# Rotary embedding on one core: one pass per 4 MB slab for the first six slabs, halves for the last two, and the sin products kept as bf16 in the slab's own memory

## The chip, the cores and the metric

The kernel runs on one core of one Trainium2 chip. The metric is the device time of one execution in microseconds; the median of five runs stands for a kernel. Beside these runs there is one profiled execution, and all durations of single instructions come from it.

## The reference

The input is 16 batches of 512 positions of 1024 numbers in fp32, seen as 16 heads of 64. Each head's first and second halves are rotated against each other with tables of cos and sin that depend on the position and on the place in the half, and that all batches and heads share.

```python
x = x.reshape(batch, seq, num_heads, head_dim)
x1, x2 = x[..., :half_dim], x[..., half_dim:]
cos = cos[None, :, None, :]
sin = sin[None, :, None, :]
rotated = np.concatenate([
    x1 * cos - x2 * sin,
    x1 * sin + x2 * cos
], axis=-1)
```

The output has the input's size: 33.55 MB are read and 33.55 MB written, and the two tables have 64 KB each.

## The kernel before, in words

Two batches make a slab: 1024 positions, eight to a partition (`rpp` is 8), so a slab is a tile of 128 partitions by 8192 fp32 numbers, 4 MB, and each partition's 32 KB are contiguous in memory. There are eight slabs, and five slots (`slots`) for them in SBUF. Five loads are issued on SP's queue at the start. A slab's result is written back over its own input in the slot, and one DMA on ScalarE's queue (L139) stores the whole slab. Load s + 5 (L65) takes the slot of slab s, so SP waits for store s to land before it issues that load.

The tables come in through two DMAs from POOL (L75), are cast to bf16 (L92), and four small matmuls with a selection matrix (L96) give every partition the rows of its own eight positions; L102 to L106 lay them out as `tab`: 8 rows of cos, then 8 rows of [sin, -sin], each row 64 numbers wide. They are used for all heads by a step of zero.

The work goes over a list of passes, `passes`: a slab has two, of four positions (`rows`) or 4096 numbers a partition each. A pass has five steps:

- ScalarE casts the half slab to bf16 into a tile `xb` (L117, in `cast`).
- VectorE multiplies `xb` by the sin rows into a tile `t2` (L130; the profile calls it t), and then `xb` by the cos rows in place (L130 again).
- VectorE adds `t2` to `xb`, with the halves of each head exchanged by a negative step (L133).
- ScalarE casts `xb` back to fp32 into the slab (L137).
- After a slab's second pass ScalarE issues the store (L139).

ScalarE's order is set by the loop: the cast of pass i + 1 stands ahead of the cast back of pass i. All engines take their instructions in order. `xb` has three buffers of 8 KB a partition and `t2` two of 8 KB; with five slabs of 32 KB that makes 200 KB a partition.

Loads go through one DMA queue and stores through another, and both run on the same 16 DMA engines.

Of the kernel before, what the change touches and what calls it, by code (L numbers as in the profile page):

```python
# [2 lines left out]

# [4 lines left out]


@with_exitstack  # L10
def kernel(
    ctx: ExitStack,
    tc: tile.TileContext,
    x: bass.AP,
    cos: bass.AP,
    sin: bass.AP,
    num_heads: int,
    out: bass.AP,
):
    nc = tc.nc  # L20
    P = nc.NUM_PARTITIONS

    batch, seq, dim = x.shape
    nh = num_heads
    hd = dim // nh
    half = hd // 2
    bf16 = mybir.dt.bfloat16
    f32 = mybir.dt.float32

    nb = 2  # L30
    slots = 5
    nslabs = batch // nb
    rpp = nb * seq // P
    W = rpp * dim
    SP = seq // rpp
    rows = 4
    PW = rows * dim
    TW = rpp * half

    out_flat = out.rearrange("b s h d -> b s (h d)")  # L40

    singles = ctx.enter_context(tc.tile_pool(name="singles", bufs=1))
    slabs = ctx.enter_context(tc.tile_pool(name="slabs", bufs=slots))
    tpool = ctx.enter_context(tc.tile_pool(name="tpool", bufs=3))
    t2pool = ctx.enter_context(tc.tile_pool(name="t2pool", bufs=2))
    psum = ctx.enter_context(tc.tile_pool(
        name="psum", bufs=1, space=bass.MemoryType.PSUM))


    def dram(t, s, a=0, n=W):  # L50
        return bass.AP(tensor=t.tensor, offset=t.offset + s * nb * seq * dim + a,
                       ap=[[W, P], [1, n]])


    def view(t, offset, *dims):
        return dataclasses.replace(t, offset=t.offset + offset,
                                   ap=[t.ap[0], *[list(d) for d in dims]])


    slab = {}  # L60


    def load(s):
        slab[s] = slabs.tile([P, W], f32, tag="slab", name="slab")
        nc.sync.dma_start(out=slab[s], in_=dram(x, s))  # L65


    load(0)


    TR = seq // P
    G = rpp // TR
    raw = singles.tile([P, 2 * TR * half], f32, tag="raw")
    for i, src in enumerate((cos, sin)):
        nc.gpsimd.dma_start(out=view(raw, i * TR * half, (1, TR * half)), in_=bass.AP(  # L75
            tensor=src.tensor, offset=src.offset,
            ap=[[TR * half, P], [1, TR * half]]))

    for s in range(1, slots):
        load(s)  # L80


    pick = singles.tile([P, G * P], bf16, tag="pick")
    nc.gpsimd.memset(pick, 0.0)  # L84
    for g in range(G):
        part = view(pick, g * P, (SP, P // SP), (1, SP))
        nc.gpsimd.affine_select(  # L87
            out=part, in_=part, compare_op=mybir.AluOpType.not_equal, fill=1.0,
            base=-g, pattern=[[0, P // SP], [-G, SP]], channel_multiplier=1)

    tab1 = singles.tile([P, 2 * TR * half], bf16, tag="tab1")
    nc.vector.tensor_copy(out=tab1, in_=raw)  # L92
    acc = psum.tile([P, 2 * TW], f32, tag="acc")
    for i in range(2):
        for g in range(G):
            nc.tensor.matmul(view(acc, i * TW + g * TR * half, (1, TR * half)),  # L96
                             view(pick, g * P, (1, P)),
                             view(tab1, i * TR * half, (1, TR * half)),
                             start=True, stop=True)

    tab = singles.tile([P, 2 * rpp * hd], bf16, tag="tab")
    nc.vector.tensor_copy(out=view(tab, 0, (hd, 2 * rpp), (1, half)),  # L102
                          in_=view(acc, 0, (half, 2 * rpp), (1, half)))
    nc.vector.tensor_copy(out=view(tab, half, (hd, rpp), (1, half)),  # L104
                          in_=view(acc, 0, (half, rpp), (1, half)))
    nc.vector.tensor_scalar_mul(  # L106
        out=view(tab, rpp * hd + half, (hd, rpp), (1, half)),
        in0=view(acc, TW, (half, rpp), (1, half)), scalar1=-1.0)


    xb = {}


    def cast(u):
        s, k = u
        xb[u] = tpool.tile([P, PW], bf16, tag="xb", name="xb")
        nc.scalar.copy(out=xb[u], in_=view(slab[s], k * PW, (1, PW)))  # L117

    passes = [(s, k) for s in range(nslabs) for k in range(rpp // rows)]
    cast(passes[0])
    for i, u in enumerate(passes):
        if i + 1 < len(passes):
            cast(passes[i + 1])
        s, k = u
        xs, xu = slab[s], xb.pop(u)
        t2 = t2pool.tile([P, PW], bf16, tag="t2")
        for t, a in ((t2, rpp * hd), (xu, 0)):
            nc.vector.tensor_mul(  # L130
                out=t, in0=xu,
                in1=view(tab, a + k * rows * hd, (hd, rows), (0, nh), (1, hd)))
        nc.vector.tensor_add(  # L133
            out=xu, in0=xu,
            in1=view(t2, half, (hd, rows * nh), (-half, 2), (1, half)))

        nc.scalar.copy(out=view(xs, k * PW, (1, PW)), in_=xu)  # L137
        if k == rpp // rows - 1:
            nc.scalar.dma_start(out=dram(out_flat, s), in_=xs)  # L139
            if s + slots < nslabs:  # L140
                load(s + slots)


# [1 line left out]
_INS = ['x', 'cos', 'sin', 'num_heads']  # L145
_OUTS = [((16, 512, 16, 64), 'float32')]

_NUMBERS = {'num_heads': 16}


# [26 lines left out]
```

## Time and profile before

| What | Value |
|---|---|
| Median of 5 runs | 162.46 us (162.37 to 163.0) |
| Profiled execution | 162.55 us |
| Span of its instructions | 160.5 us |
| VectorE busy | 111.3 us, 69% of the span, 52 instructions |
| ScalarE busy | 114.8 us, 72% of the span, 33 instructions |
| Moved by DMA | 67.24 MB, mean 419 GB/s over the span |
| Load, issue to landing, median | 27.5 us |
| Store, issue to landing, median | 28.5 us |
| Issue of the stores 0 to 7 | 34.46, 48.64, 62.82, 77.00, 93.77, 113.13, 132.50, 146.68 us |
| Issue of the loads 5, 6, 7 | 59.03, 78.57, 97.86 us |

The span is the time from the program's first instruction to its last event; the profiled execution's own time is about 2 us longer, and that difference lies around the span. A share of the span is a mean over stages, so an engine at 70% may be the limit in one stage and idle in another. The time from issue to landing of a load or a store contains the time in which it lies in its queue behind others: a slab's packets themselves take about 10 us when its queue has the DMA engines alone, and about 19 us when loads and stores share them.

### The profile page before, as it was taken

The page shows a single profiled execution, that of the slowest core. Times are in us where ns is not written, and L with a number is a line of the kernel's source. Part 1 is how long each engine was busy: PE and PEld are TensorE (multiplying, and loading weights), DVE is VectorE, ACT ScalarE, POOL GpSimd, SP SyncE. Part 2 cuts the span into 40 slices and gives each one's busy share as a digit, 9 for nine tenths or more (in the row PEclk, how much of TensorE's full clock was granted, in tenths as well). Part 3 has the DMA queues.
Part 4 walks back from the last instruction along what each step waited for, and adds up shares of the span by engine and source line. Part 5 has one row for each costly group of instructions (what it writes and reads, how often), then busy time and mean ns, then how long its engine had stood idle before and what let it go on. Part 6 is the DMA issues. An engine that isn't in the chain of part 4 may idle for free.

```text
span 160.5 us, 182 instructions
## 1 busy us (share of the span) xinstructions
PE 0.6 (0%) x4; PEld 0.4 (0%) x4; DVE 111.3 (69%) x52; ACT 114.8 (72%) x33; POOL 2.3 (1%) x9
## 2 busy tenths in 40 slices
PE   0010000000000000000000000000000000000000
PEld 0000000000000000000000000000000000000000
DVE  0003799999999999999997499906998089960000
ACT  3006939899999999999994999159990799735000
POOL 5000000000000000000000000000000000000000
DMA  7999999999999999999999999999999999999994
GB/s 237 425 417 392 482 433 392 433 474 351 441 392 441 474 392 392 474 441 392 466 449 392 441 457 408 441 457 408 400 482 425 392 474 441 392 474 441 392 457 196
DMA packets 2368, 67.24 MB, mean 419 GB/s; under 512 B 288, under 2 KB 288, under 8 KB 320
## 3 DMA queue, kind: packets, MB, share of 16 engines
q1 hardware_dynamic: 1152, 33.55, 49.4%
q10 hardware_dynamic: 1152, 33.55, 48.4%
q0 software_dynamic: 64, 0.13, 0.2%
HBM read 33.69 MB, written 33.55 MB: 419 GB/s over the span
## 4 chain that ended last, share of the span: by engine, by line
DMA 47%; ACT 25%; DVE 13%; issue 6%; ACTq 0%; SPq 0%
DMA slab<-in_x_dram 25%; DMA out_dram<-slab 22%; ACT slab L137 16%; ACT xb L117 9%; DVE xb L130 4%; DVE t L130 4%; DVE xb L133 4%; ACTq L137 0%; SPq L65 0%
## 5 line engine op out<-in xcount | busy, mean ns | idle before, releaser
L117 ACT CAST xb<-slab 128x4096 bf16<-128x4096 f32 x16 | 57.6, 3604 | 27.1 <-DMA slab<-in_x_dram 27.1
L137 ACT CAST slab<-xb 128x4096 f32<-128x4096 bf16 x16 | 57.7, 3605 | 4.1 <-DVE xb L133 3.9
L130 DVE TENSOR_TENSOR t<-xb,tab 128x4096 bf16<-128x4096 bf16 x16 | 36.7, 2291 | 18.7 <-ACT xb L117 18.3
L133 DVE TENSOR_TENSOR xb<-xb,t 128x4096 bf16<-128x4096 bf16 x16 | 36.7, 2292 | 0.5
L130 DVE TENSOR_TENSOR xb<-xb,tab 128x4096 bf16<-128x4096 bf16 x16 | 36.7, 2291 | 0.5
L92 DVE CAST tab<-raw 128x256 bf16<-128x256 f32 x1 | 0.3, 294 | 11.2 <-DMA raw<-in_sin_dram 11.2
L117 ACT ACT_TABLE_LOAD x1 | 1.3, 1283 | 0.7 <-PEq L158 0.7
L102 DVE CAST tab<-acc 128x512 bf16<-128x512 f32 x1 | 0.7, 691 | 0.7 <-PE acc L96 0.7
L75 POOL DMA_DIRECT2D raw<-in_cos_dram x1 | 0.7, 677 | 0.8 <-POOLq L158 0.8
L96 PE MATMUL acc<-tab,pick 128*128 128x128 bf16 x4 | 0.6, 300 | 11.5 <-DVE tab L92 11.5
L87 POOL TENSOR_SCALAR_AFFINE_SELECT pick<-pick 128x128 bf16<-128x128 bf16 x2 | 0.5, 289 | 0.1
L75 POOL DMA_DIRECT2D raw<-in_sin_dram x1 | 0.5, 537 | 0.0
L96 PEld LDWEIGHTS <-pick 128*128 128x128 bf16 x4 | 0.4, 124 | 11.4 <-issue 8.3
L106 DVE TENSOR_SCALAR tab<-acc 128x256 bf16<-128x256 f32 x1 | 0.4, 415 | 0.0
L104 DVE CAST tab<-acc 128x256 bf16<-128x256 f32 x1 | 0.4, 414 | 0.0
L84 POOL MEMSET pick<- 128x256 bf16 x1 | 0.3, 331 | 0.0
L158 POOL MEMSET const-float32-0.0<- 128x1 f32 x1 | 0.1, 99 | 0.2 <-issue 0.2
L158 POOL MEMSET const-bfloat16-1.0<- 128x1 bf16 x1 | 0.1, 102 | 0.0
L158 POOL MEMSET const-uint8-127<- 128x1 uint8 x1 | 0.1, 102 | 0.0
L158 POOL MEMSET const-float32-1.0<- 128x1 f32 x1 | 0.1, 99 | 0.0
## 6 DMA issues: line engine op xcount, KB each, us to landing
slab<-in_x_dram SPq DMA_DIRECT2D x8, 4096.0 KB, 27.5
out_dram<-slab ACTq DMA_DIRECT2D x8, 4096.0 KB, 28.5
raw<-in_cos_dram POOLq DMA_DIRECT2D x1, 64.0 KB, 7.2
raw<-in_sin_dram POOLq DMA_DIRECT2D x1, 64.0 KB, 9.2
```

Source lines behind the costliest of these rows:

```text
L75: nc.gpsimd.dma_start(out=view(raw, i * TR * half, (1, TR * half)), in_=bass.AP(tensor=src.tensor, offset=src.offset, ap=[[TR * half, P], ...
L84: nc.gpsimd.memset(pick, 0.0)
L87: nc.gpsimd.affine_select(out=part, in_=part, compare_op=mybir.AluOpType.not_equal, fill=1.0, base=-g, pattern=[[0, P // SP], [-G, SP]], c ...
L96: nc.tensor.matmul(view(acc, i * TW + g * TR * half, (1, TR * half)), view(pick, g * P, (1, P)), view(tab1, i * TR * half, (1, TR * half)) ...
L102: nc.vector.tensor_copy(out=view(tab, 0, (hd, 2 * rpp), (1, half)), in_=view(acc, 0, (half, 2 * rpp), (1, half)))
L104: nc.vector.tensor_copy(out=view(tab, half, (hd, rpp), (1, half)), in_=view(acc, 0, (half, rpp), (1, half)))
L106: nc.vector.tensor_scalar_mul(out=view(tab, rpp * hd + half, (hd, rpp), (1, half)), in0=view(acc, TW, (half, rpp), (1, half)), scalar1=-1.0)
L117: nc.scalar.copy(out=xb[u], in_=view(slab[s], k * PW, (1, PW)))
L130: nc.vector.tensor_mul(out=t, in0=xu, in1=view(tab, a + k * rows * hd, (hd, rows), (0, nh), (1, hd)))
L133: nc.vector.tensor_add(out=xu, in0=xu, in1=view(t2, half, (hd, rows * nh), (-half, 2), (1, half)))
L137: nc.scalar.copy(out=view(xs, k * PW, (1, PW)), in_=xu)
L158: nc = _bacc.Bacc("TRN2", target_bir_lowering=False, num_devices=1)
```

## The change

The first six slabs are done in one pass of 8192 numbers a partition; the last two keep two passes of 4096 each. `xb` becomes a tile of a whole slab (16 KB a partition) with two buffers, allocated when a slab's first pass begins. The tile `t2` goes: the sin product is written as bf16 into the first half of the bytes of the very part of the slab that has just been cast, and the cast back overwrites it with the result. A slab is still loaded by one DMA and stored by one DMA, in five slots. The tables' loads, from POOL, are the same in both kernels.

```diff
-    rows = 4
-    PW = rows * dim
...
-    tpool = ctx.enter_context(tc.tile_pool(name="tpool", bufs=3))
-    t2pool = ctx.enter_context(tc.tile_pool(name="t2pool", bufs=2))
+    xpool = ctx.enter_context(tc.tile_pool(name="xpool", bufs=2))
...
     def cast(u):
-        s, k = u
-        xb[u] = tpool.tile([P, PW], bf16, tag="xb", name="xb")
-        nc.scalar.copy(out=xb[u], in_=view(slab[s], k * PW, (1, PW)))
+        s, r, n = u
+        if r == 0:
+            xb[s] = xpool.tile([P, W], bf16, tag="xb", name="xb")
+        nc.scalar.copy(out=view(xb[s], r * dim, (1, n * dim)),
+                       in_=view(slab[s], r * dim, (1, n * dim)))
...
-    passes = [(s, k) for s in range(nslabs) for k in range(rpp // rows)]
+    passes = []
+    for s in range(nslabs):
+        n = rpp if s < nslabs - 2 else rpp // 2
+        passes += [(s, r, n) for r in range(0, rpp, n)]
...
     cast(passes[0])
-    for i, u in enumerate(passes):
+    for i, (s, r, n) in enumerate(passes):
         if i + 1 < len(passes):
             cast(passes[i + 1])
-        s, k = u
-        xs, xu = slab[s], xb.pop(u)
-        t2 = t2pool.tile([P, PW], bf16, tag="t2")
+        xs = view(slab[s], r * dim, (1, n * dim))
+        xu = view(xb[s], r * dim, (1, n * dim))
+
+        t2 = view(slab[s].bitcast(bf16), 2 * r * dim, (1, n * dim))
         for t, a in ((t2, rpp * hd), (xu, 0)):
             nc.vector.tensor_mul(
                 out=t, in0=xu,
-                in1=view(tab, a + k * rows * hd, (hd, rows), (0, nh), (1, hd)))
+                in1=view(tab, a + r * hd, (hd, n), (0, nh), (1, hd)))
         nc.vector.tensor_add(
-            out=xu, in0=xu,
-            in1=view(t2, half, (hd, rows * nh), (-half, 2), (1, half)))
+            out=xu, in0=xu, in1=view(t2, half, (hd, n * nh), (-half, 2), (1, half)))
 
-        nc.scalar.copy(out=view(xs, k * PW, (1, PW)), in_=xu)
-        if k == rpp // rows - 1:
-            nc.scalar.dma_start(out=dram(out_flat, s), in_=xs)
+        nc.scalar.copy(out=xs, in_=xu)
+        if r + n == rpp:
+            nc.scalar.dma_start(out=dram(out_flat, s), in_=slab[s])
             if s + slots < nslabs:
                 load(s + slots)
```

## The prediction

> **What bounds the kernel now.** I read the forty slices first, because they say at once whether any engine or the transfers are busy throughout.
>
> ```profile
> DVE  0003799999999999999997499906998089960000
> ACT  3006939899999999999994999159990799735000
> DMA  7999999999999999999999999999999999999994
> GB/s 237 425 417 392 482 433 392 433 474 351 441 392 441 474 392 392 474 441 392 466 449 392 441 457 408 441 457 408 400 482 425 392 474 441 392 474 441 392 457 196
> ```
>
> VectorE and ScalarE have holes; the 16 DMA engines have none between the first and the last slice. The table of DMA queues puts a price on this.
>
> ```profile
> q1 hardware_dynamic: 1152, 33.55, 49.4%
> q10 hardware_dynamic: 1152, 33.55, 48.4%
> q0 software_dynamic: 64, 0.13, 0.2%
> ```
>
> Together 98.0% of 160.5 us. q1 holds the loads, q10 the stores, the same bytes each. The stores' share is 0.484 x 160.5 = 77.7 us, or 9.7 us for each of eight 4 MB slabs; if loads cost the same, 16 slabs need 155.4 us. So only 160.5 - 155.4 = 5.1 us of the span is not plain transfer. In the trace's packet records the first packet starts at 1.75 and the last ends at 159.2; that makes 1.75 + 1.25 us at the two ends and about 2.1 us inside. Next, stretches of the span side by side tell where those 2.1 us are (columns: stretch, length, busy time by engine, clock, DMA share, GB/s).
>
> ```profile
> 10.00:35.00 25.00, 0.59 (x4) 0.32 (x3) 19.36 (x12) 18.40 (x6) 0.00 (x0) 1.00 1.02 440
> 35.00:40.00 5.00, 0.00 (x0) 0.00 (x0) 4.59 (x3) 5.00 (x2) 0.00 (x0) 1.00 0.96 360
> 60.00:125.00 65.00, 0.00 (x0) 0.00 (x0) 54.18 (x24) 52.38 (x15) 0.00 (x0) 1.00 1.00 432
> 125.00:150.00 25.00, 0.00 (x0) 0.00 (x0) 13.75 (x6) 17.83 (x5) 0.00 (x0) 1.00 0.99 429
> ```
>
> Loads alone (10 to 35), both directions (60 to 125) and stores alone (125 to 150) run at one rate, within what cutting at a packet's start costs; it doesn't matter how the two are mixed. The only dip is at 35 to 40, where the first store, issued at 34.46, joins the loads. By packets: a 32 KB packet takes 1.213 us in the steady state, and what packets took beyond this, for each engine, was 0.71 us at 0 to 4, 0.64 us at 36 to 40, 0.18 us at 56 to 60, and about 0.1 us over 4 to 34; the tables' packets are another 0.3 us. That is the 2.1 us. After 60 it is nil.
>
> The chain of waits and the end of ScalarE's timeline say what the last store waited for.
>
> ```profile
> DMA 47%; ACT 25%; DVE 13%; issue 6%; ACTq 0%; SPq 0%
> ```
>
> ```profile
> 125.36 3.60 ACT L117 CAST xb<-slab 128x4096 bf16<-128x4096 f32 x1 [5.15 <-DMA slab<-in_x_dram]
> 143.04 3.60 ACT L137 CAST slab<-xb 128x4096 f32<-128x4096 bf16 x1 [3.46 <-DVE xb L133]
> 146.68 0.34 ACTq L139 DMA_DIRECT2D out_dram<-slab  x1
> ```
>
> The chain's 38% of ACT and DVE must not be taken for time to be had: it is a path through one slab's work, with the DMA engines full beside it. Slab 7 lands at 125.34, its store is issued at 146.68, and its packets start at 148.95, 9.68 us after those of slab 6, which is the plain pitch. The last store came just in time; an earlier issue ends nothing earlier.
>
> **What the Trainium skill says.** "DMA: Bandwidth & Descriptors", section Queues, rings and completion order: each DMA engine takes turns among the rows that have work, packet by packet. The trace agrees: with both queues active each moves about 216 GB/s, alone 433. The same page under Specifications gives 435 GB/s as the ceiling on the SBUF side; 432 here is that ceiling. "SBUF — State Buffer", section Who interferes with whom: DMAs have ports of their own and don't contend with compute engines; packets of 1.213 us with VectorE at 9 tenths agree. "VectorE: DVE Perf Modes", section on the perf-mode tier table: a bf16 tensor_tensor in SBUF runs at two elements a cycle; here 4096 elements took 2.291 us, which is that.
>
> **The change part by part.** The order of instructions of the changed program on each engine gives the counts; the durations come from the costliest groups of the kernel before (busy us, mean ns of one, idle time before them).
>
> ```profile
> L117 ACT CAST xb<-slab 128x4096 bf16<-128x4096 f32 x16 | 57.6, 3604 | 27.1 <-DMA slab<-in_x_dram 27.1
> L137 ACT CAST slab<-xb 128x4096 f32<-128x4096 bf16 x16 | 57.7, 3605 | 4.1 <-DVE xb L133 3.9
> L130 DVE TENSOR_TENSOR t<-xb,tab 128x4096 bf16<-128x4096 bf16 x16 | 36.7, 2291 | 18.7 <-ACT xb L117 18.3
> ```
>
> 1. Fewer, longer instructions. 32 casts of 4096 become 12 of 8192 and 8 of 4096; 48 vector operations become 18 of 8192 and 12 of 4096. No cast of 8192 is in the trace: at most 2 x 3.605 = 7.21 us, at least the 186 ns + 0.833 ns an element of "ScalarE: Activation LUTs" (What ACT_TABLE_LOAD costs), 7.01 us; its 3.60 at 4096 is the trace's. A vector operation of 8192: at most 4.58, and by (cycles + 151)/0.96 GHz of the vector page's TRN2 errata section, which gives 2.291 at 4096, 4.42 us. I take 7.01 and 4.42. VectorE's slab goes from 13.7 to 13.3 us, ScalarE's from 14.4 to 14.0. Busy time falls by 2 to 3 us on each, and none of it is on the path that sets the end: the DMA engines need 2 x 9.7 = 19.4 us a slab.
>
> 2. The first store goes out later. Slab 0 lands at 13.53 as before. Cast 13.55 to 20.6, three operations to 34.0, cast back to 41.0, store at about 41.1 instead of 34.46. These 6.6 us are covered by loads: five are queued from the start, and at 9.7 us each and a first end at 13 they last to 51.8 alone. SP's queue holds nothing but loads, so nothing else is passed.
>
> 3. What follows in the load queue. Load 5 waits for store 0's landing. First store packet 4.0 us after its issue (34.46 to 38.49), so 45.1. Load 4, begun at 42.2, has by then moved 2.9 us at the full rate, the rest goes at half: done at 58.7. Store 0 does its last 2.9 us at the full rate: data out at 61.6, landed near 62; before, 58.94. Load 5 is issued then, with first packets 1.0 us later (as load 0) to 4 us later (as store 0). So from 58.7 to 63 or 66 the load queue is empty, which before it never was (load 5 issued at 59.03, load 4's packets end at 65.7). Store 1, issued at 55.2, fills the engines: 6.4 us of cover. Without it the gap would cost up to its 4 to 7 us.
>
> 4. The rest. Sharing from 64: load 5 ends at 83.4, load 6 at 102.8, load 7 at 122.2, landed 123.8 (before 125.34): what loads gained early, stores give up. ScalarE keeps its order: the next pass's cast stands ahead of this pass's cast back, so it can block on a load while a finished slab waits. Stores 2 to 4 are issued near 69, 84 and 99, each before the one ahead has ended.
>
> 5. The end. Slabs 6 and 7 go in halves, as all did before. Cast of 7's first half at 123.8; behind it on ScalarE stand the cast back of 6's second half, the second cast, and two casts back; the last of these waits for VectorE till 141.5. Store 7 is issued at about 145.2, 1.5 us ahead of before, with store 6's packets lasting to about 149. No gain: the queue is full.
>
> 6. Sin products in the slab's memory. The write must follow the cast that reads that memory, but the product waits for that very cast's output anyway; the cast back already waits for the addition. The halves touch disjoint bytes, and each half's first product has its own wait on ScalarE, so none waits for the other half's cast. Slots stay five, so no load may start earlier. Cost: nothing, hidden by DMA; point C tells when not.
>
> 7. Tables: POOL's list is the same in both programs, line numbers apart. Nothing.
>
> Sum against the profiled execution: span 160.5; ends unchanged; 155.4 of transfer unchanged; the start's 0.71, the tables' 0.3 and the first store's 0.64 recur (it meets load 4 instead of 3); 56 to 60's 0.18 may go, since stores then run alone; the restart of the load queue is unknown: at least 0 (stores fill the engines), at most the 0.71 that the cold start cost. A gain from it is excluded, as packets at 1.213 us are the fastest seen. I take 0.2. Net 0.0, so 160.5, and with the 2.05 us around it 162.55; the five runs' median, 162.46, lies 0.1 below. Forecast 162.5.
>
> **The rivals.**
> A, forecast, 0.60: full DMA engines, 162.5. For it: one rate in all mixes. Against it: only that bubbles at changes of mix exist at all.
> B, slower, 0.20: load 5 restarts an empty queue at 63 to 66 and its first packets stretch as at the cold start. 162.5 - 0.2 + 0.71 = 163.0; it decides from a bubble of about 0.5. For it: load packets, never store packets, stretched at 36 to 40. Against it: engines had stores to move, and after 60 changes of mix cost nothing.
> C, slower, 0.05: vector operations on slab memory are slower, and VectorE bounds. It starts at 20.6; with p us a slab the last store goes out at 20.6 + 8p + 3.7, and must by 146.7: it decides from p = 15.3, 15% over 13.3. If the two operations that touch the slab fell to one element a cycle, 8.69 us each, p = 21.8 and the time about 20.6 + 174.4 + 3.7 + 14 + 2 = 215. Against it: same type, contiguous, same ports.
> D, faster, 0.15: the bubble of the first store (0.64) and that at 56 to 60 (0.18) don't recur: 162.5 - 0.8 = 161.7. For it: both came where a store met loads, and the second meeting now has no loads. Against: the first still meets them.
>
> **How the numbers follow.** 0.2% of 162.46 is 0.32 us, about what a measurement of this kernel can tell from no change. A gives same, B and C slower, D faster: 0.15, 0.60, 0.25. The range takes A and most of B and D: 162.0 to 163.2.
>
> **What would show it.** Right: DMA at 9 in all slices from 1 to 38, last store issued near 145, store 0 near 41, load 5 near 62, ACT casts of about 7.0 us and products of 4.42 us, span 160.5. Wrong: a DMA slice under 9 inside the span (near 64 for B), vector operations over 5.1 us (C), stores issued later than the end of the one ahead, or a GB/s dip that is missing at 40 to 46 (D).

## The result, and the profile after

| | before | changed |
|---|---|---|
| Median | 162.80 us (162.30 to 163.35, 80 runs) | 162.38 us (161.45 to 164.45, 43 runs) |
| Ratio, 95% interval | | 0.9978 (0.9968 to 0.9988) |
| Profiled execution, and its span | 162.55, 160.5 us | 162.71, 160.9 us |

The changed kernel is faster by 0.22%, and no change was forecast. The profiled execution doesn't show it: it took 0.16 us longer than that of the kernel before. Ratios and the means below leave out the runs 1.5% and more above their own kernel's fastest (one of the changed kernel, one of it with ScalarE padded, 15 of 22 of the kernel before with store 0 held back); medians don't.

From the changed kernel's page, its span, four of the rows of forty slices and its DMA queues:

```profile
span 160.9 us, 153 instructions
DVE  0003089999979997999799589958829599940000
ACT  3006939559899899989995999079996999653000
DMA  7999999999989999999999999999999999999993
GB/s 236 415 424 391 497 415 391 472 440 391 448 334 505 407 391 497 415 391 497 399 391 497 415 391 489 424 391 481 432 391 472 440 391 456 456 391 440 472 391 147
q1 hardware_dynamic: 1152, 33.55, 49.2%
q10 hardware_dynamic: 1152, 33.55, 48.3%
```

The DMA row is full from slice 1 to slice 38, apart from one digit 8 at 44 to 48 us, where the first store now meets the loads and the rate falls to 334 GB/s. The queues take 78 to 79 us each, as before. Stretches of the changed kernel (stretch, length, busy time by engine, clock, DMA share, GB/s):

```profile
10.00:35.00 25.00, 0.59 (x4) 0.32 (x3) 15.98 (x8) 15.00 (x3) 0.00 (x0) 1.00 1.02 440
40.00:50.00 10.00, 0.00 (x0) 0.00 (x0) 8.61 (x3) 9.55 (x3) 0.00 (x0) 1.00 1.03 419
60.00:125.00 65.00, 0.00 (x0) 0.00 (x0) 53.83 (x16) 55.23 (x11) 0.00 (x0) 1.00 1.01 435
```

The rates are those of before; only the dip has moved, from 36 to 40 us to 44 to 48 us. The groups of the changed kernel, shapes kept apart, and the end of its timeline on ScalarE:

```profile
L114 ACT CAST xb<-slab 128x8192 bf16<-128x8192 f32 x6 | 42.1, 7019 | 17.6 <-DMA slab<-in_x_dram 16.4 <-ACT slab L140 1.3
L134 DVE TENSOR_TENSOR xb<-xb,tab 128x8192 bf16<-128x8192 bf16 x6 | 26.5, 4424 | 0.2
L134 DVE TENSOR_TENSOR slab<-xb,tab 128x8192 bf16<-128x8192 bf16 x6 | 26.5, 4424 | 13.2 <-ACT xb L114 13.2
```

```profile
142.69 3.61 ACT L140 CAST slab<-xb 128x4096 f32<-128x4096 bf16 x1 [3.47 <-DVE xb L137]
146.32 0.34 ACTq L142 DMA_DIRECT2D out_dram<-slab  x1
```

A product written into the slab takes what one written into `xb` takes. Store 7 goes out 0.36 us earlier than before, and it doesn't matter.

So the transfers did what was forecast. To see where the 0.2% is, every run is split. Each run lists its time and its span (to 0.1 us); the difference is what lies around the span. Over the comparison runs of all experiments, and for the changed kernel also those of the result:

| | runs | time, mean | span, mean | around the span, mean |
|---|---|---|---|---|
| before | 184 | 162.75 us | 160.70 us (standard error 0.02) | 2.046 us (0.006) |
| changed | 58 | 162.45 us | 160.68 us (0.07) | 1.776 us (0.004) |

Within these errors the spans are equal. The 0.27 us lie outside them, and the profile's page doesn't show what happens there. A stretch laid past the end of the span does: first the kernel before, then the changed one.

```profile
160.90:163.00 2.10, 0.00 (x0) 0.00 (x0) 0.00 (x0) 0.00 (x0) 0.00 (x0) 1.00 0.03 8
```

```profile
160.90:163.00 2.10, 0.00 (x0) 0.00 (x0) 0.00 (x0) 0.00 (x0) 0.00 (x0) 1.00 0.00 0
```

8 GB/s over 2.1 us are 16 KB. In the packet records they are two packets of 8192 bytes of the instruction queue, at 162.29 and 162.30 us. The changed kernel has none there.

### The profile page after: what moved, and what is told of

Its sections match the earlier page's. It is cut to its first block, busy times and chain, and to the rows that moved or that the text cites. A ratio compares the mean times of both kernels' runs of the same rounds, so it can differ in the third digit from the quotient of the medians.

```text
span 160.9 us, 153 instructions
## 1 busy us (share of the span) xinstructions
PE 0.6 (0%) x4; PEld 0.4 (0%) x4; DVE 108.7 (68%) x34; ACT 113.5 (71%) x21; POOL 2.3 (1%) x9
## 4 chain that ended last, share of the span: by engine, by line
DMA 42%; ACT 34%; DVE 13%; issue 1%; ACTq 0%; SPq 0%
DMA slab<-in_x_dram 24%; DMA out_dram<-slab 18%; ACT slab L140 17%; ACT xb L114 16%; DVE slab L134 4%; DVE xb L137 4%; DVE xb L134 4%; ACTq L142 0%; ACTq L140 0%; SPq L62 0%
## 5 line engine op out<-in xcount | busy, mean ns | idle before, releaser
L114 ACT CAST xb<-slab 128x8192 bf16<-128x8192 f32 (+1 forms) x10 | 56.5, 5653 | 24.9 <-DMA slab<-in_x_dram 23.6
L140 ACT CAST slab<-xb 128x8192 f32<-128x8192 bf16 (+1 forms) x10 | 56.5, 5652 | 7.2 <-DVE xb L137 7.2
L134 DVE TENSOR_TENSOR slab<-xb,tab 128x8192 bf16<-128x8192 bf16 (+1 forms) x10 | 35.7, 3572 | 21.3 <-ACT xb L114 21.3
L137 DVE TENSOR_TENSOR xb<-xb,slab 128x8192 bf16<-128x8192 bf16 (+1 forms) x10 | 35.7, 3572 | 0.3
L134 DVE TENSOR_TENSOR xb<-xb,tab 128x8192 bf16<-128x8192 bf16 (+1 forms) x10 | 35.7, 3571 | 0.3
```

The costliest lines, as they stand in the source:

```text
L114: nc.scalar.copy(out=view(xb[s], r * dim, (1, n * dim)), in_=view(slab[s], r * dim, (1, n * dim)))
L134: nc.vector.tensor_mul(out=t, in0=xu, in1=view(tab, a + r * hd, (hd, n), (0, nh), (1, hd)))
L137: nc.vector.tensor_add(out=xu, in0=xu, in1=view(t2, half, (hd, n * nh), (-half, 2), (1, half)))
L140: nc.scalar.copy(out=xs, in_=xu)
```

## The experiments

Two theories were put up first. J (joins): the DMA engines lose time where one queue joins the other, and the change loses less. W (work): longer instructions, or the products' place, quicken the transfers. Later came N (the gain lies outside the span and follows the number of instructions) and F (it follows where an engine's instruction stream ends). "Excess" below is what load and store packets took beyond 1.213 us each, for one engine, from the packet records. The diffs show the main lines of each edit, with comments added; a ratio is the run's time to that of the kernel before, with its 95% interval.

**The changed kernel again.** No edit.

> The changed kernel again, unaltered. Theory J (joins): beyond 16 slabs of plain packets the DMA engines lose time only where one queue joins the other; the changed kernel loses less because the hand-over from store 0 to store 1 no longer meets loads, and the last of the 16 engines to finish sets the end. Expected under J: ratio to before 0.996 to 0.999, single runs spread over 161.5 to 163.4, and in the packet records either all engines end near 158.6 or one or two of them about one packet (1.2 us) later. Theory W (work): the longer vector and scalar instructions, or the sin product's place in the slab, quicken the transfers: same ratio, but no engine loses less at joins than before.

0.9986 (0.9966 to 1.0005), runs from 161.72 to 163.43: as expected, though this interval alone doesn't exclude 1. Its trace is read further down, beside two others.

**Halves everywhere.**

```diff
-        n = rpp if s < nslabs - 2 else rpp // 2
+        n = rpp // 2
```

> The changed kernel with halves for all eight slabs, so the first store goes out near 34.5 again, while the sin products stay in the slab's memory and xb stays a whole-slab tile. Theory J: back at the kernel before, ratio 1.000 within 0.1%, a dip in the DMA rate at 36 to 40 and a second small one at 56 to 60. Theory W, if the place of the products is what counts: ratio 0.998 as the changed kernel; if the instruction length is what counts: 1.000.

1.0000 (0.9989 to 1.0011), store 0 at 34.5, excess at the first store 0.88 us. So the place of the products is worth nothing that shows, within 0.11%. This fits J and leaves W only the instructions' length.

**The kernel before with store 0 held back.**

```diff
         if i + 1 < len(passes):
             cast(passes[i + 1])
+        if i == 3:
+            store(0)   # kept behind that cast on ScalarE
```

> The kernel before with one edit: store 0 is held back in ScalarE's queue behind the cast of slab 2's first half, so it goes out near 41.5 instead of 34.46; all instructions, buffers and halves are those of before. Theory J: ratio 0.997 to 0.999, like the changed kernel, first dip at 43 to 48, no excess at the hand-over from store 0 to store 1. Theory W: 1.000.

The store went out at 37.5, not 41.5. Median 165.47 us, runs from 162.21 to 167.16; ratio 1.0034 (1.0002 to 1.0065). J had no such scatter in it. Another execution of this kernel:

> A second look at the kernel before with store 0 held back, most of whose runs took 164.3 to 167.2 us and a few 162.2 to 162.6. J: the lost 2 to 5 us lie in stretched packets or in a gap where a queue joins or restarts, after store 0's issue. W: they lie in scalar or vector instructions or in waits for them.

This execution took 164.78 us. Fifteen of its DMA engines end their last packet between 158.55 and 159.04 us and one at 161.30. The mean excess of the 16 engines doesn't tell this: it hides the one that the store's completion waits for. Where that engine lost its 2.3 us is not cleanly readable, since the records don't name the engine.

**The changed kernel with store 0 held back to 48** (`keep` pins the program's order on ScalarE for the first slabs).

```diff
         keep(nc.scalar.copy(out=xs, in_=xu), s < 3)
-        if r + n == rpp:
+        if r + n == rpp and s > 0:
+            if s == 1:
+                store(0)
             store(s)
```

> The changed kernel with store 0 held back further, behind the cast back of slab 1, so it goes out near 48.2 and its packets begin near 50.5 to 52, when load 4's packets are ending. Theory J: the bubble of the first store (about 0.6 us per engine) shrinks or goes, engines end near 158.0, ratio 0.994 to 0.997. Theory W: 0.998 as the changed kernel. If holding the store back drains the DMA engines (a gap near 52), the ratio is above 1.000.

Store 0 went out at 47.3, its packets start at 51.9, as load 4 ends. Ratio 0.9975 (0.9965 to 0.9985). But the first store's excess is 0.64 us and the engines end at 158.76 in the mean, not 158.0. The ratio lies between J's 0.994 to 0.997 and W's 0.998, and its interval reaches both; the mechanism J asked for is missing. What lies around the span is 1.77 us, as in the changed kernel. This is the lowest median of all, 162.26 us, and its interval covers the changed kernel's ratio, so it isn't shown to be better.

**One queue for loads and stores**, in the changed kernel and in the kernel before.

```diff
-            nc.scalar.dma_start(out=dram(out_flat, s), in_=slab[s])
-            if s + slots < nslabs:
-                load(s + slots)
+            store(s)       # on SP; after stores 1 to 3 also load(s + 4)
```

> The changed kernel with all loads and stores on one queue (SP's) in the order L0 to L4, S0, S1, L5, S2, L6, S3, L7, S4 to S7, so loads and stores never share the DMA engines. Theory J (the time beyond 16 slabs of plain packets is lost where a second queue joins): no packet over 1.26 us after the start, all 16 engines end within 0.7 us of each other near 158.0, ratio to before 0.990 to 0.994, spread of single runs no more than that of the kernel before. Theory W (longer instructions or the products' place): 0.998 as the changed kernel. If taking turns is needed for the full rate, or SP's waits leave gaps, the ratio is over 1.

> The kernel before, in halves and with its own t2 tiles, with all loads and stores on SP's queue in the same order as in the run with one queue of the changed kernel. Theory J: the same time as that run within 0.1%, 0.990 to 0.994 of before. Theory W: 1.000, or slower than that run by 0.2%.

1.1006 (1.0989 to 1.1023) and 1.0306 (1.0287 to 1.0324). The new order delayed the last slabs' casts, and the DMA engines ran dry. Stretches of the changed kernel on one queue:

```profile
140.00:145.00 5.00, 0.00 (x0) 0.00 (x0) 0.82 (x1) 4.09 (x2) 0.00 (x0) 1.00 0.00 0
155.50:165.50 10.00, 0.00 (x0) 0.00 (x0) 6.07 (x3) 7.21 (x2) 0.00 (x0) 1.00 0.00 0
```

So the totals answer another question. Up to there the run can still be read: the fourteenth slab's packets end at 140.06 us, against 139.86 in the kernel before, and the first store behind the loads costs 0.61 us of excess although there is one queue. J's joining of a second queue is not the cause of that loss.

**Tables on ScalarE's queue.**

```diff
-        nc.gpsimd.dma_start(out=view(raw,
+        nc.scalar.dma_start(out=view(raw,
```

> The changed kernel with the two table loads on ScalarE's DMA queue in place of POOL's, so store 0 is not the first DMA of its queue. If the bubble at store 0 is a queue's first use: no slow packets near 44, ratio 0.994 to 0.996. If it is the joining of a second stream, as J says: slow load packets near 44 as in the changed kernel, ratio 0.997 to 0.999.

1.0093 (1.0074 to 1.0112). The tables landed at 13.2 and 23.1 us instead of 8.5 and 11.1, and store 0 went out at 46.1. Its excess was 0.62 us, so it is not the queue's first use. Most of the time was lost later:

```profile
65.00:70.00 5.00, 0.00 (x0) 0.00 (x0) 3.98 (x2) 5.00 (x2) 0.00 (x0) 1.00 1.00 328
75.00:80.00 5.00, 0.00 (x0) 0.00 (x0) 4.97 (x2) 4.76 (x1) 0.00 (x0) 1.00 1.02 387
```

At the time when load 5 restarts an empty load queue, packets of both queues stretch: 1.24 us an engine at 62 to 72 and 0.64 at 72 to 84. DMA share 1.00 beside 328 GB/s is the sign of it: busy engines that move less. That the restart causes it is not shown; the changed kernel restarts its load queue at the same time without it.

**Which slabs in one pass.**

```diff
-        n = rpp if s < nslabs - 2 else rpp // 2      # both edits replace this line
+        n = rpp if s == 0 else rpp // 2               # first slab alone
+        n = rpp if 1 < s < nslabs - 2 else rpp // 2   # middle slabs alone
```

> The changed kernel with only slab 0 in one pass and all others in halves, so store 0 goes out near 41 and all later work has the short instructions. Theory J2 (the gain belongs to where the first store falls among the loads, and the last of 16 DMA engines sets the end): 0.997 to 0.999 of before, most engines end near 158.6. Theory W (the long instructions of all slabs): 1.000.

> The changed kernel with slabs 0 and 1 in halves as well, so only slabs 2 to 5 are done in one pass and store 0 goes out near 34.5. Theory J2: 1.000 within 0.1%, first slow load packets at 36 to 40, as in the kernel before. Theory W: 0.998 to 0.999.

1.0015 (0.9999 to 1.0031) and 1.0010 (1.0001 to 1.0018): neither part alone brings the gain, against J and W both. (Split as above, the first has 1.85 us around a longer span, 161.06 us in the mean; the second has 2.18 us around a span of 160.70.)

**A write to HBM at the start.**

```diff
+    probe = singles.tile([P, 128], f32, tag="probe")
+    nc.gpsimd.memset(probe, 0.0)
+    nc.scalar.dma_start(out=dram(out_flat, nslabs - 1, 0, 128), in_=probe)
```

> The changed kernel with a small store of zeros (512 bytes a partition, into the place that store 7 overwrites later) on ScalarE's queue at the very start, so that store 0 is not the first write to HBM. If the 0.6 us an engine near 44 are the price of a first write: no slow packets there, ratio 0.993 to 0.996. If they are the price of store data meeting loads: slow packets near 44 as before, ratio 0.997 to 1.000.

1.0037 (1.0023 to 1.0051), first-store excess 0.65 us: not the price of a first write. The ratio is above both expectations; the mean span is 161.42 us, and why isn't shown.

**The changed kernel once more.**

> One more look at the changed kernel, whose single runs spread from 161.5 to 163.4 us. J2: the time of this execution follows its slowest DMA engine (last packet's end + 3.0 us), while the mean end of the 16 engines stays within 158.5 to 158.9. Rival: all engines are later or earlier together.

162.30 us. The three traces of the changed kernel and those of the kernel before, by the end of each engine's last packet, from the packet records:

| execution | time | first engine | mean of 16 | last engine |
|---|---|---|---|---|
| before | 162.55 us | 158.63 | 158.90 | 159.23 |
| changed | 162.71 us | 158.50 | 158.75 | 159.71 |
| changed, second | 162.79 us | 158.61 | 158.88 | 159.79 |
| changed, third | 162.30 us | 158.58 | 158.73 | 159.32 |

In the changed kernel's traces time minus last engine is 3.0 us each time, so the last engine sets an execution's time. That fits the changed kernel's wider scatter (standard deviation of the span 0.6 us against 0.2), but it is not its gain: the mean of the engines is 0.02 to 0.17 us earlier than in the kernel before, the last one 0.1 to 0.6 us later. In the kernel before time minus last engine is 3.3 us, and this 0.3 led to the split above. With equal spans J and W have no gain left to explain.

**Padding the changed kernel** with instructions that do nothing useful, while both engines wait for the first load:

```diff
+    pad = singles.tile([P, 4], f32, tag="pad")
+    nc.gpsimd.memset(view(pad, 0, (1, 2)), 0.0)
+    for _ in range(18):
+        nc.vector.memset(view(pad, 2, (1, 2)), 0.0)
+    for _ in range(12):
+        nc.scalar.copy(out=view(pad, 1, (1, 1)), in_=view(pad, 0, (1, 1)))
```

> The changed kernel with 18 memsets of two numbers on VectorE and 12 copies of one number on ScalarE at the start, where both engines wait for the first loads; VectorE and ScalarE then have about as many instructions as in the kernel before, and the transfers are untouched. Theory N (the gain lies outside the span: the part around it is 1.77 us with few instructions and 2.02 to 2.09 with many): part around the span 2.0 to 2.1 us, span 160.5 to 160.8 in the mean as the changed kernel, ratio to before 0.999 to 1.001. Theory J (the transfers lose less): around the span 1.77, ratio 0.998.

> The changed kernel with the 18 small memsets on VectorE alone. Theory N with VectorE's stream as the one that ends late: around the span 2.0 to 2.1 us. N with ScalarE's stream: 1.77. J: 1.77.

> The changed kernel with the 12 small copies on ScalarE alone. Theory N with ScalarE's stream as the one that ends late: around the span 1.9 to 2.1 us, as in the kernels with 39 rows on ScalarE. N with VectorE's: 1.77. J: 1.77.

Around the span: 1.769, 1.773 and 1.768 us with both, VectorE's and ScalarE's padding. With 184 instructions, two more than the kernel before, it stays where it was: N falls. With VectorE padded, a packet of the instruction queue does come, but inside the span, at 130.6 us (both) and 128.3 (VectorE alone). Ratios 1.0003 (0.9988 to 1.0018), 1.0010 (0.9990 to 1.0030) and 0.9981 (0.9962 to 1.0001), from spans of 161.04, 161.13 and 160.75 us that scatter by 0.5 to 0.7.

**Padding the kernel before**, with 12 of each kind, then one kind alone.

> The kernel before with 12 memsets of two numbers on VectorE and 12 copies of one number on ScalarE added at the start, where both wait. Theory F (what costs is a packet of the instruction queue after the span's end, that is, where the end of an engine's instruction stream falls; in the kernel before two such packets come at 162.3 us): the added instructions draw that fetch forward into the span, so the part around the span falls from 2.05 to about 1.77 us though there are more instructions, span 160.6 to 160.8 in the mean, ratio 0.998 to 0.999. Theory N (the number of instructions): around 2.05 or more, ratio 1.000 or above.

> The kernel before with the 12 memsets on VectorE alone. F, if VectorE's stream has the late fetch: around 1.77 to 1.85 us, one of the two late packets gone; if ScalarE's: 2.05. N: 2.05 or more.

> The kernel before with the 12 copies on ScalarE alone. F, if ScalarE's stream has the late fetch: around 1.77 to 1.85 us, one of the two late packets gone; if VectorE's: 2.05. N: 2.05 or more.

Around the span: 1.793 us with both, 2.011 with VectorE's alone, 2.054 with ScalarE's alone; the kernel before on the same chip 2.027. More instructions, and the part around the span falls by 0.23 us. The page's DMA queues of the run with both paddings have a line that the kernel before has not,

```profile
q14 instruction: 2, 0.02, 0.0%
```

and past its span nothing moves. Past that of the run with VectorE's padding alone one 8 KB packet still comes (3 GB/s over 2.5 us). First both paddings, then VectorE's:

```profile
161.00:163.50 2.50, 0.00 (x0) 0.00 (x0) 0.00 (x0) 0.00 (x0) 0.00 (x0) 1.00 0.00 0
```

```profile
161.00:163.50 2.50, 0.00 (x0) 0.00 (x0) 0.00 (x0) 0.00 (x0) 0.00 (x0) 1.00 0.01 3
```

With both paddings the two packets come at 84.7 and 135.4 us, inside the span. With one kind of padding one of them comes inside and the other stays outside, and one is enough for nearly the whole price; so neither padding alone brought the 1.77 to 1.85 us that was expected for one of the two. This is what F says. The ratio with both was missed: 0.9998 (0.9990 to 1.0006) where 0.998 to 0.999 was expected, because this span is 160.90 us, 0.2 longer than that of the kernel before. The copies had also moved store 0 to 36.95; whether that, or the two packets among the full transfers, lengthened the span isn't shown. The others gave 1.0003 (0.9992 to 1.0014) and 1.0007 (0.9997 to 1.0017).

The part around the span by kernel, with the packets in each one's trace (instructions: all, then VectorE's and ScalarE's, waits and issues included):

| kernel | instructions | packets of the instruction queue after the span | around, us |
|---|---|---|---|
| changed; store at 48; tables on ScalarE's queue; early write | 152 to 155 (49; 41 to 43) | none | 1.77 to 1.78 |
| changed, one queue | 162 (49; 38) | none | 1.79 |
| changed, padded (three) | 184 (67; 53), 171 (67; 41), 166 (49; 53) | none | 1.77 |
| before, both padded | 207 (72; 71) | none | 1.79 |
| first slab whole | 184 (64; 56) | one | 1.85 |
| halves everywhere | 189 (67; 59) | one | 1.96 |
| before, one padded (two) | 194 (72; 59), 195 (60; 71) | one | 2.01, 2.05 |
| before; with store 0 held back | 182 (60; 59), 183 (60; 60) | two | 2.05, 2.04 |
| before, one queue | 193 (60; 57) | one | 2.26 |
| middle slabs whole | 165 (55; 47) | none recorded | 2.18 |

By each engine's own count the packets fall into order. With 49 instructions on VectorE none comes; with 60 one comes after the span, with 64 at 161.3 us, with 67 at 128 to 131, with 72 at 83.7 to 84.7. On ScalarE none comes up to 57, one after the span at 59 and 60, and one at 135 to 136 with 71. (The records don't name a packet's engine. This sorting is read from the paddings of one engine alone, and fits every trace but that of the last row.)

The records also show why a late packet counts. In the seven traces in which the last such packet ends after the last recorded semaphore update, its end, counted from the span's start, lies 0.240 to 0.248 us above the recorded time (162.79 against 162.55 in the kernel before): the recorded time ends with that packet. In eleven traces with none after the span it is that last update that keeps a fixed distance to the recorded time, 0.12 to 0.14 us above it. With the first slab whole the packet ends at 161.63, ahead of the last update at 162.36, and costs least. Whether anything but the end of the count waits for a late packet isn't shown.

The last row doesn't fit and stays open: its VectorE count lies between "none" and "after the span", and its last update lies 0.27 us below the recorded time instead of above it, with nothing recorded later. The size in the row above it stays open too (four runs, 2.04 to 2.43). The others are in the order that F asks for.

## Why the prediction was right and wrong

The working of the span held nearly line by line. A cast of 8192 took 7.02 us (7.01 taken) and a vector operation 4.42 us (4.42). Store 0 was issued at 41.09 (41.1), landed at 62.41 (62), load 5 was issued at 62.49 and had its first packets at 66.5 (63 to 66). Store 1 at 55.48 (55.2) covered the empty load queue. Load 7 landed at 124.98 (123.8), store 7 went out at 146.32 (145.2).

The bubbles, as the prediction calls the packets' excess: the first store's recurred, 0.61 us an engine (0.64); that at 56 to 60 was gone, as one reading had it; the restart cost 0.03 us at 62 to 72 and 0.07 at 72 to 84, less than the 0.2 taken. One named sign of being wrong did appear, a slice under 9, but at 44 to 48, where the first store's bubble was expected, and not near 64. The net of the span is 160.68 - 160.70, nil as forecast. (The bubbles that the prediction lists add up to 1.93 us and not quite to its 2.1; the forecast doesn't rest on the rest.)

Rival B, the restart, did not decide here; in the run with the tables on ScalarE's queue more than the 0.71 us allowed for it was lost at that time, 1.24 us an engine. Rival C is out: 13.3 us a slab, not 15.3. Rival D had the sign right by luck: the bubbles it named did not bring the gain. There is luck in the forecast's number too: 162.5 is close to the measured 162.38, but it was built on a median of five runs, 162.46, that lay 0.34 below the 162.80 of 80 runs.

The step that failed is the term "the 2.05 us around it", taken over unchanged from the profiled execution and added to the new span. It measured 1.776 us, and these 0.27 us are 0.17% of the time, which lies within the interval of the 0.22%. The prediction counted the instructions that the change takes away as engine time alone. They also have to be fetched. "Runtime: NRT & Kernel Launch", section Instruction fetch mechanics, says that an engine's instructions are fetched in blocks by a DMA queue that its sequencer drives, and calls the cost of crossing into the next block mostly hidden. The traces agree in that a fetch inside the span (the two packets at 84.7 and 135.4 us) adds nothing to the part around it, 1.793 us; they differ where it comes after the span: there the recorded time ends with it, 0.23 to 0.27 us later. The change took 29 instructions out of the program, and the two late fetches went with them.

The scatter was not forecast either. The sum was made with an engine's mean loss, 0.64 us and so on, but an execution ends with its slowest engine, and in the changed kernel that one is up to 1 us behind the mean. This is also why its single profiled execution stands on the wrong side of the median: its last engine ended at 159.71 us, the mean at 158.75.

## What to carry to other kernels

Split every run into its span and what lies around it before looking for a cause inside; for a kernel whose span is full of transfers, 0.2% can come from the other part. When a change removes or adds instructions, ask where the ends of the engines' instruction streams come to lie: a fetch after the span cost about a quarter of a microsecond here. One inside it added nothing around the span, but that it is free isn't shown: the padded kernels' spans were 0.06 to 0.45 us longer than without padding, and none of them was shown to be faster than its unpadded kernel. And with 16 engines behind one completion, add up the slowest one, not the mean.

## What the runs showed of the hardware

- The first store after a run of loads costs each DMA engine about 0.6 us (0.59 to 0.96 over the kernels), whether it comes at 36 or at 50 us, on its own queue or on the loads', as a first write or not. Its cause stays open.
- While a load queue that had run empty beside stores restarted (62 to 72 us), packets lost 0.03 us an engine in the changed kernel and 1.24 us with the tables on ScalarE's queue. Why is open.
- The tables' 256 packets of 512 bytes on a hardware queue took turns with 32 KB load packets: the second 64 KB table landed at 23.1 us there, and at 11.1 us from POOL's queue, in packets of 4096 bytes.
- With two packets of the instruction queue after the span, the part around it was 2.046 us; with both drawn into the span by padding, 1.793 us.
- Of 16 DMA engines with equal shares one can end 2.3 us after all others (161.30 against 159.04 us).
